# A fourth raw weight buffer, loads one unit earlier, and one scratch tag shared by three uses

## The chip, the cores and the metric

The kernel runs on one core of one Trainium2 chip. The metric is the device time of one launch in microseconds; of the kernel before there are three timed runs, 1531.43, 1519.66 and 1522.27 us, with a median of 1522.27 us. A separate execution was profiled: it took 1527.95 us, of which the profile shows a span of 1526.2 us.

## The reference

Two layers of a hybrid encoder over 256 tokens of width 2048 in float32, each a pre-norm mixer with a residual, then a final RMS norm. Cut to what matters:

```python
u = rms_norm(x, norm_g)
qk, v, o, z_a, ig, fg, xb, z_b = split(u @ w_in)          # w_in: 2048 x 12304
qk = silu(causal_dwconv(qk, qk_conv))                      # 4 taps
q, k = split(qk); k = k * DK_A ** -0.5
h = mlstm_chunkwise(q, k, v, i_pre, log_f)                 # 8 heads, DK 128, DV 256
y_a = group_norm(h * sigmoid(o)) * head_norm_g * silu(z_a)
xc = causal_dwconv(xb, lru_conv_w) + lru_conv_b
y_b = rg_lru(xc, w_a, b_a, w_x, b_x, lam) * silu(z_b)      # gates: sigmoid(xc @ w_a), sigmoid(xc @ w_x)
return x + concat([y_a, y_b]) @ w_out                      # w_out: 4096 x 2048
```

The weights of a layer are read once, some 100 MB in float32 and its `w_out` 33 MB; the products must hold nearly float32's accuracy.

## The kernel before, in words

**Weights.** All weights are laid out in HBM as units of 128 x 2048 floats (1 MB). A unit is loaded by SyncE's queue into a raw buffer (`load_unit`, pool `wraw`, tag `raw`, three buffers). Each half of it (128 x 1024) is then split in two: ScalarE casts the raw half to the TensorE's float32r format, `wH` (L337), and VectorE subtracts to get the rest, `wL` (L338, which the profile shows under the helper's line L187). The pairs H and L have four buffers (pool `wsp`). TensorE multiplies each half as three products, H by H, H by L and L by H (L361): twelve matmuls of 512 columns a half, 24 a unit. A raw buffer is free when `wL` of its second half is done.

**Order.** The main loop at the end of `tile_trunk` walks over the halves. For the half n it first prepares (casts and subtracts) up to half n + 3, and ahead of each preparation it issues loads. With `(nprep + 5) // 2` it has, ahead of the first half of unit m, loaded up to unit m + 2; that load takes the buffer of unit m - 1, whose last subtraction has just been issued. After each half `pump` advances generators that hold the rest of the work (convolutions, gates, scores, the recurrence); a generator that yields "wait" lets the next one go on. Every engine carries out its own instructions in the order in which the program puts them; ScalarE and VectorE thus share one line each between the splits of the weights and the rest.

**Groups.** Each layer has four head groups g. Of a group the projections o, qk, v, xb, z and zb are made, some in another order, then the gates of the recurrence; chunks of `w_out` of the group before are put between. For two of the projections (z of g = 2, o of g = 3) a seven-product block scheme is used, whose summed weights are made by DMAs that add in HBM: GpSimd issues them (`w_d`, L1032), and SyncE's queue reads the sums back as raw units (`raw<-w_d`, L297). A unit of this scheme makes six matmuls a half, twelve in all (`ps_b`, L1095 to L1097). Turning a token-major result into channels goes through HBM too: four DMAs `moved<-blk` on SyncE's queue (L481), one `fr<-moved` on GpSimd's (L482).

**Scratch tiles.** Tiles of the pool `work` with one tag share one buffer: a new tile waits until all that reads the old one is done. The diff is about two tags of 8 KB a partition each. `qs` holds `qks`, the split q and k of a group (L667; read by the score matmuls `ps_S`, L682 and L684), and at the end of layer 0 `tokblk`, the token block and its transpose for the chunks c = 1 and 3 (L942). `xcs` holds `scs`, the rows of the input and forget gates once a layer (L541; last read by GpSimd's copies into `at`, L591, after which the program notes `("aT", l)`), and `xcs`, the split convolution of xb of a group (L768; read by the gate matmuls `ps_gt`, L795).

Of the kernel before, what the change touches and what calls it, by code (L numbers as in the profile page):

```python
# [9 lines left out]
F32 = mybir.dt.float32  # L10
# [83 lines left out]
def tile_trunk(ctx, tc, x, xt, par, gw, gb, ws, final_g, out):  # L94
# [1 line left out]
    V, S, G, PE = nc.vector, nc.scalar, nc.gpsimd, nc.tensor  # L96

    const = ctx.enter_context(tc.tile_pool(name="const", bufs=1))
    wraw = ctx.enter_context(tc.tile_pool(name="wraw", bufs=3))
    wsp = ctx.enter_context(tc.tile_pool(name="wsp", bufs=4))  # L100
    act = ctx.enter_context(tc.tile_pool(name="act", bufs=1))
    work = ctx.enter_context(tc.tile_pool(name="work", bufs=1))
# [547 lines left out]
    def qk_post(l, g, acc):  # L650
        bg.append(e_gen(l, g))
        fr = to_channels(l, acc)

        def gen():
            for _ in range(LANDING):
                yield "wait"
            ch = joined(fr)
            yield 0.3
            qc = work.tile([P, 4, T], F32, tag="c4", name="qc", bufs=2)
            sg = work.tile([P, 4, T], F32, tag="sC", name="qsg")  # L660
            for ct in range(4):
                conv(ch, qc, ct, O_QKW + 4 * (8 * (ct % 2) + 2 * g + ct // 2), l, None)
                yield 1.2
            S.activation(out=sg, in_=qc, func=AF.Sigmoid)
            tt_(qc, qc, sg, ALU.mult)
            yield 1.2
            q = work.tile([P, 4, 2, T], F32R, tag="qs", name="qks")  # L667
            S.copy(out=q[:, :, 0, :], in_=qc)
            tt_(q[:, :, 1, :], qc, q.bitcast(F32)[:, :, 0, :], ALU.subtract)
            yield 1.2  # L670
            for _ in range(3):
                yield "wait"
            while any((k, l, g) not in st for k in ("E", "v", "so")):
                yield "wait"
            E, em, so, (vH, vL) = st["E", l, g], st["em", l], st["so", l, g], st["v", l, g]
            Pt = work.tile([P, 2, 384], F32, tag="ch", name="Pt")
            for h in range(2):
                pa, pb = aux("ps_S"), aux("ps_S")
                kH, kL = q[:, 2 * h + 1, 0], q[:, 2 * h + 1, 1]
                for ps, ss_, ts_1 in ((pa, slice(0, 128), slice(0, 256)), (pb, slice(128, 256), slice(128, 256))):  # L680
                    n_ = ts_1.stop - ts_1.start
                    PE.matmul(ps[:, 0 : 2 * n_].rearrange("p (a t) -> p a t", a=2), kH[:, ss_], q[:, 2 * h, :, ts_1],  # L682
                              start=True, stop=False, skip_group_check=True)
                    PE.matmul(ps[:, 0:n_], kL[:, ss_], q[:, 2 * h, 0, ts_1], start=False, stop=True,  # L684
                              skip_group_check=True)
                for ps, o_, n_ in ((pa, 0, 256), (pb, 256, 128)):
                    S.copy(out=Pt[:, h, o_ : o_ + n_], in_=ps[:, n_ : 2 * n_])
                    tt_(Pt[:, h, o_ : o_ + n_], ps[:, 0:n_], Pt[:, h, o_ : o_ + n_], ALU.add)
                stt(Pt[:, h, :], Pt[:, h, :], DK_SCALE, E[:, h, :], ALU.mult, ALU.mult)
                yield 0.5  # L690
            PH = work.tile([P, 2, 384], F32R, tag="sD", name="PH")
            PL = work.tile([P, 2, 384], F32R, tag="sC", name="PL")
            S.copy(out=PH, in_=Pt)
            tt_(PL, Pt, PH.bitcast(F32), ALU.subtract)
            yield 1.0
            for _ in range(3):
                yield "wait"
            hh = work.tile([P, 2, 2, 256], F32, tag="sE", name="hh")
            mv = small.tile([P, 2, 2, 2], F32, tag="mv", name="mv", bufs=1)
            for h in range(2):  # L700
                pns = [aux("ps_n") for _ in range(2)]
                for t in range(2):
                    o = pns[t][:, 0:258]
                    a = slice(P * t, P * t + P)
                    mm3(o, PH[:, h, a], PL[:, h, a], vH[:, 0, h, :], vL[:, 0, h, :], last=t == 0)
                    if t == 1:
                        mm3(o, PH[:, h, 256:384], PL[:, h, 256:384], vH[:, 1, h, :], vL[:, 1, h, :], first=False)
                for t in range(2):
                    pn = pns[t]
                    dn = small.tile([P, 1], F32, tag="dn", name="dn")  # L710
                    stt(dn, pn[:, 256:257], -1.0, em[:, t, 2 * g + h : 2 * g + h + 1], ALU.mult, ALU.max)
                    tt_(dn, dn, pn[:, 256:257], ALU.max)
                    V.reciprocal(out=dn, in_=dn)
                    stt(hh[:, t, h, :], pn[:, 0:256], dn, so[:, t, 256 * h : 256 * h + 256], ALU.mult, ALU.mult)
                    bs = small.tile([P, 6], F32, tag="bs", name="bs")
                    V.bn_stats(out=bs, in_=hh[:, t, h, :])
                    V.bn_aggr(out=mv[:, t, h, :], in_=bs)
                    yield 1.1
            sd = small.tile([P, 2, 2], F32, tag="sd", name="sd", bufs=1)
            order(S.activation(out=sd, in_=mv[:, :, :, 1], func=AF.Sqrt, bias=epst), st["wH"])  # L720
            V.reciprocal(out=sd, in_=sd)
            for hd in range(2):
                for t in range(2):
                    ts_(hh[:, t, hd, :], hh[:, t, hd, :], mv[:, t, hd, 0:1], ALU.subtract, sd[:, t, hd : hd + 1],
                        ALU.mult)
            st["hn", l, g] = hh
            yield 1.0
        bg.append(gen())
# [30 lines left out]
    def xb_post(l, g, acc):  # L759
        fr = to_channels(l, acc)  # L760

        def gen():
# [2 lines left out]
            ch = joined(fr)  # L765
            yield 0.3
            xc = work.tile([P, 4, T], F32, tag="c4", name="xc", bufs=2)
            xs = work.tile([P, 4, 2, T], F32R, tag="xcs", name="xcs")  # L768
            for ct in range(4):
                tix = 4 * g + ct  # L770
                conv(ch, xc, ct, O_LW + 4 * tix, l, pars[:, l, O_LB + tix : O_LB + tix + 1])
                yield 1.2
            for b in range(2):
                sl_ = slice(2 * b, 2 * b + 2)
                S.copy(out=xs[:, sl_, 0, :], in_=xc[:, sl_, :])
                tt_(xs[:, sl_, 1, :], xc[:, sl_, :], xs.bitcast(F32)[:, sl_, 0, :], ALU.subtract)
                yield 0.6
# [142 lines left out]
    def out_chunk(l, g, c):  # L920
# [9 lines left out]
        def postfn():  # L930
# [8 lines left out]
                new_xT()  # L939
                load_gw(l + 1)  # L940
            if c % 2:
                two = work.tile([P, 2, 1024], F32, tag="qs", name="tokblk")  # L942
                tok = two[:, 0].rearrange("p (m c t j) -> p m c t j", m=4, c=4, t=2)
                blk = two[:, 1].rearrange("p (m n) -> p m n", m=4)
            else:
# [374 lines left out]
    for n, hf in enumerate(order_):  # L1320
        st["n"] = n
        while nprep < len(order_) and nprep <= n + AHEAD:
            while st["nload"] < len(order_) // 2 and st["nload"] <= (nprep + 5) // 2:
                load_unit(order_[2 * st["nload"]])
            prepare(order_[nprep])
            nprep += 1
# [107 lines left out]
```

## Time and profile before

| | |
|---|---|
| median of three runs | 1522.27 us (1519.66 to 1531.43) |
| profiled execution, and its span | 1527.95 us, 1526.2 us |
| TensorE busy | 1489.4 us, 98% |
| VectorE busy | 1140.2 us, 75% |
| ScalarE busy | 966.2 us, 63% |
| DMA moved | 383.44 MB, 251 GB/s in the mean |
| mean granted TensorE clock | 0.993 |

Busy time is what the profile saw an engine work; matmuls are pipelined and overlap in it, so that TensorE can be busy without being at its best pace. A wait names an engine and what it waited for, in total microseconds, the number of times and the longest. In rows of the timeline, what stands in brackets is the idle time of the engine just ahead of the instruction and who ended it. A row of a window holds the stretch, its length, then busy time and count for TensorE, its weight loads, VectorE, ScalarE and GpSimd, the granted TensorE clock, the share of the 16 DMA engines and GB/s.

### The profile page before, as it was taken

What the parts mean: (1) busy time and instruction counts of PE and PEld (TensorE: products, weight loads), DVE (VectorE), ACT (ScalarE), POOL (GpSimd) and SP (SyncE); (2) the same over time, 40 slices, a digit from 0 to 9 for tenths busy, and PEclk for the clock granted to TensorE, in tenths of its full rate; (3) what the DMA queues carried; (4) which work ended last, traced back from release to release, by engine and by line L of the source; (5) the groups of instructions that cost most, each with busy time, mean ns of one, the idle gap of its engine ahead of it and who ended that gap; (6) DMA issues with size and microseconds to landing.
All of it is one profiled execution on the core that took longest, in us unless ns stands there. A gap on an engine that the chain in (4) does not pass through costs nothing.

```text
span 1526.2 us, 18815 instructions
## 1 busy us (share of the span) xinstructions
PE 1489.4 (98%) x6782; PEld 1229.3 (81%) x6782; DVE 1140.2 (75%) x1634; ACT 966.2 (63%) x1258; POOL 107.5 (7%) x186
## 2 busy tenths in 40 slices
PE   9999989999999999999999998999999999999997
PEld 7887768878788878788888787788887888788886
DVE  5879967668867875587867899775986578757785
ACT  6656765557556675568575558654675567755675
POOL 0020010010000100000000200100000000000002
PEclk9999999999999999999999999999999999999999
DMA  9779787897879998976785674978778688677773
GB/s 339 275 256 264 244 284 213 260 288 250 243 279 304 259 279 273 298 238 241 255 296 193 210 263 152 291 216 263 235 247 286 227 236 238 224 236 264 245 265 121
DMA packets 100014, 383.44 MB, mean 251 GB/s; under 512 B 10944, under 2 KB 31440, under 8 KB 76880
## 3 DMA queue, kind: packets, MB, share of 16 engines
q1 hardware_dynamic: 83504, 327.41, 61.6%
q0 software_dynamic: 13952, 50.35, 15.4%
q10 hardware_dynamic: 2464, 4.47, 0.8%
q8 instruction: 53, 0.87, 0.2%
q14 instruction: 41, 0.34, 0.1%
HBM read 344.95 MB, written 62.41 MB: 267 GB/s over the span
## 4 chain that ended last, share of the span: by engine, by line
PE 66%; DMA 12%; DVE 10%; issue 8%; ACT 3%; SPq 0%; POOL 0%; DVEq 0%; ACTq 0%; POOLq 0%
PE acc L361 54%; DMA raw<-in_ws_dram 8%; DVE wL L187 4%; PE ps_gt L795 2%; ACT wH L337 2%; PE acc L374 1%; DMA nb<-nG_d 1%; PE ps_b L1097 1%; PE ps_b L1096 1%; PE ps_b L1095 1%; DMA fr<-moved 1%; DVE xc L190 1%; PE acc L1193 1%; PE acc L1191 1%; PE acc L1192 1%
## 5 line engine op out<-in xcount | busy, mean ns | idle before, releaser
L361 PE MATMUL acc<-wH,x_s 128*128 128x512 f32 x2752 | 860.9, 391 | 7.3 <-ACT wH L337 7.3
L187 DVE TENSOR_TENSOR wL<-raw,wH 128x1024 fp32r<-128x1024 f32 (+1 forms) x556 | 663.3, 1204 | 267.2 <-ACT wH L337 265.5
L337 ACT CAST wH<-raw 128x1024 fp32r<-128x1024 f32 (+1 forms) x556 | 569.7, 1037 | 373.3 <-PE acc L361 252.1
L361 PEld LDWEIGHTS acc<-wH,x_s 128*128 128x128 f32 x2752 | 518.3, 189 | 116.8 <-ACT wH L337 10.2
L361 PE MATMUL acc<-wL,x_s 128*128 128x512 f32 x1376 | 538.6, 392 | 12.5 <-DVE wL L187 12.4
L361 PEld LDWEIGHTS acc<-wL,x_s 128*128 128x128 f32 x1376 | 259.5, 189 | 73.9 <-DVE wL L187 20.4
L361 PE MATMUL acc<-wH,yaH 128*128 128x512 f32 x224 | 87.6, 391 | 0.0
L361 PE MATMUL acc<-wH,yaL 128*128 128x512 f32 x224 | 87.4, 390 | 0.0
L361 PE MATMUL acc<-wL,ybH 128*128 128x512 f32 x224 | 87.3, 390 | 0.0
L361 PE MATMUL acc<-wH,ybL 128*128 128x512 f32 x224 | 87.3, 390 | 0.0
L361 PE MATMUL acc<-wL,yaH 128*128 128x512 f32 x224 | 87.2, 389 | 0.0
L361 PE MATMUL acc<-wH,ybH 128*128 128x512 f32 x224 | 87.2, 389 | 0.0
L478 DVE STREAM_TRANSPOSE blk<-tok 128x1024 f32<-128x1024 f32 x33 | 40.9, 1240 | 21.3 <-ACT tok L468 21.3
L482 POOL DMA_DIRECT2D fr<-moved x34 | 19.0, 560 | 466.6 <-DMA moved<-blk 335.7
L795 PE MATMUL ps_gt<-xcs,wH 128*128 128x256 f32 x256 | 46.9, 281 | 3.2 <-DVE xcs L187 2.0
L361 PEld LDWEIGHTS acc<-wH,ybL 128*128 128x128 f32 x224 | 42.0, 188 | 9.0 <-DVE ybL L187 0.3
L361 PEld LDWEIGHTS acc<-wL,ybH 128*128 128x128 f32 x224 | 42.0, 188 | 8.9 <-DVE wL L187 0.3
L361 PEld LDWEIGHTS acc<-wH,yaL 128*128 128x128 f32 x224 | 42.0, 188 | 8.8
L361 PEld LDWEIGHTS acc<-wH,yaH 128*128 128x128 f32 x224 | 42.2, 188 | 8.4
L361 PEld LDWEIGHTS acc<-wH,ybH 128*128 128x128 f32 x224 | 42.0, 188 | 8.6
L361 PEld LDWEIGHTS acc<-wL,yaH 128*128 128x128 f32 x224 | 42.1, 188 | 8.3
L190 DVE SCALAR_TENSOR_TENSOR qc<-ch,pars,qc 128x255 f32<-128x255 f32 (+2 forms) x96 | 41.4, 478 | 5.0 <-ACT qc L450 4.7
(234 smaller groups left out, 1580.5 us busy)
## 6 DMA issues: line engine op xcount, KB each, us to landing
raw<-in_ws_dram SPq DMA_DIRECT2D x164, 1024.0 KB, 6.2
raw<-in_ws_dram SPq DMA_DIRECT2D x190, 512.0 KB, 6.2
fr<-moved POOLq DMA_DIRECT2D x34, 512.0 KB, 5.8
moved<-blk SPq DMA_DIRECT2D x132, 128.0 KB, 2.8
w_d<-in_ws_dram POOLq DMA_DIRECT2D x32, 512.0 KB, 12.1
raw<-w_d SPq DMA_DIRECT2D x16, 1024.0 KB, 6.7
x_d<-stage POOLq DMA_DIRECT2D x24, 512.0 KB, 6.6
w_d<-in_ws_dram SPq DMA_DIRECT2D x16, 512.0 KB, 7.7
```

Source lines behind the costliest of these rows:

```text
L187: return V.tensor_tensor(out=o, in0=a, in1=b, op=op)
L190: return V.scalar_tensor_tensor(out=o, in0=a, scalar=s, in1=b, op0=op0, op1=op1)
L337: st["wH"] = S.copy(out=H[:, o], in_=r[:, o])
L361: st["mm"] = PE.matmul(o, a_[:, kt, P * t : P * t + P], W[:, k], start=b, stop=z)
L374: PE.matmul(ps[:, ct, T * part : 2 * T], W[:, k, P * ct : P * ct + P], moving, start=first and k == 0 and part == 0, stop=last and k == 3 ...
L478: V.transpose(out=blk.rearrange("p m n -> p (m n)"), in_=tok.rearrange("p m c t j -> p (m c t j)"))
L482: i0 = back.dma_start(out=fr.rearrange("p a c t i -> p a (c t i)"), in_=moved)
L795: PE.matmul(o, W[:, ib, jl], xs[:, ib, a, :], start=j == 0 and i == 0 and W is Hv and a == 0, stop=i == 1 and W is Lv, skip_group_check=True)
L1095: PE.matmul(box["b"], aH, Hv[:, k], start=kp == 0 and k == 0, stop=False)
L1096: PE.matmul(box["b"], aH, Lv[:, k], start=False, stop=False)
L1097: PE.matmul(box["b"], aL, Hv[:, k], start=False, stop=kp == 3 and k == 1)
L1191: PE.matmul(o, yH[:, kt, tsl], Hv[:, k, cs], start=start and k == 0, stop=False)
```

## The change

The pool of raw buffers gets four buffers, and the loop loads one unit further ahead: ahead of the first half of unit m, up to unit m + 3. Its buffer is again that of unit m - 1. The 8 KB a partition for it come from the tag `qs`, which is given up: `qks` and `tokblk` now use the tag `xcs`, with `scs` and the split convolution. So that tiles of this tag follow each other in a set order, the generator that makes `qks` goes on only once `("aT", l)` is noted, and the one that makes the split convolution of a group asks for its tile after the convolution instead of before, and only once the scores of the group have been issued.

```diff
-    wraw = ctx.enter_context(tc.tile_pool(name="wraw", bufs=3))
+    wraw = ctx.enter_context(tc.tile_pool(name="wraw", bufs=4))
...
-            q = work.tile([P, 4, 2, T], F32R, tag="qs", name="qks")
+            while ("aT", l) not in st:
+                yield "wait"
+            q = work.tile([P, 4, 2, T], F32R, tag="xcs", name="qks")
...
+            st["scores", l, g] = True
             PH = work.tile([P, 2, 384], F32R, tag="sD", name="PH")
...
             xc = work.tile([P, 4, T], F32, tag="c4", name="xc", bufs=2)
-            xs = work.tile([P, 4, 2, T], F32R, tag="xcs", name="xcs")
             for ct in range(4):
                 tix = 4 * g + ct
                 conv(ch, xc, ct, O_LW + 4 * tix, l, pars[:, l, O_LB + tix : O_LB + tix + 1])
                 yield 1.2
+            while ("scores", l, g) not in st:
+                yield "wait"
+            xs = work.tile([P, 4, 2, T], F32R, tag="xcs", name="xcs")
...
-                two = work.tile([P, 2, 1024], F32, tag="qs", name="tokblk")
+                two = work.tile([P, 2, 1024], F32, tag="xcs", name="tokblk")
...
-            while st["nload"] < len(order_) // 2 and st["nload"] <= (nprep + 5) // 2:
+            while st["nload"] < len(order_) // 2 and st["nload"] <= (nprep + 7) // 2:
                 load_unit(order_[2 * st["nload"]])
```

The order of the instructions follows. On SyncE's queue, around the fifth group of DMAs that hand a block over (`moved<-blk`), early in layer 0 (`raw` is a raw unit, L306 and L297 two ways of loading one), before:

```order
L306 DMA raw<-in_ws_dram 128x2048
L481 DMA moved<-blk 32x4x256 x4
L306 DMA raw<-in_ws_dram 128x2048
L297 DMA raw<-in_ws_dram 128x2048
L306 DMA raw<-in_ws_dram 128x2048 x3
```

and now:

```order
L306 DMA raw<-in_ws_dram 128x2048
L481 DMA moved<-blk 32x4x256 x4
L297 DMA raw<-in_ws_dram 128x2048
L306 DMA raw<-in_ws_dram 128x2048 x3
```

The unit that was loaded right behind the hand-over is now loaded ahead of it, and the one of L297 stands in its place: the sequence of loads is shifted by one unit against everything else on this queue.

On TensorE, where the loads of those rows are used (`ps_b` is the block scheme, whose unit is the one of L297; `acc<-wH,x_s` behind its first row belongs to the unit after it), before:

```order
L361 MATMUL acc<-wH,x_s 128x512
L1095 MATMUL ps_b<-wH,x_s 128x512
L361 MATMUL acc<-wH,x_s 128x512
L1096 MATMUL ps_b<-wL,x_s 128x512
L1097 MATMUL ps_b<-wH,x_s 128x512
```

and now:

```order
L361 MATMUL acc<-wH,x_s 128x512
L1100 MATMUL ps_b<-wH,x_s 128x512
L1101 MATMUL ps_b<-wL,x_s 128x512
L1102 MATMUL ps_b<-wH,x_s 128x512
L1100 MATMUL ps_b<-wH,x_s 128x512
```

The first matmul of the next unit stood second in the block unit's twelve; now it follows the last of them.

On GpSimd, at the switch from layer 0 to layer 1 (`scs` are the gate rows of layer 1, `gwp` the gate weights, `fr` a block that comes back as channels, `vL` a part of v), before:

```order
L935 DMA x_d_98<-stage 128x1024
L935 DMA x_d_99<-stage 128x1024
L566 MEMSET scs 64x256
L482 DMA fr<-moved 128x1024
L641 MEMSET vH 128x4x2
L482 DMA fr<-moved 128x1024 x2
L521 MEMSET gwp 128x832 x2
L482 DMA fr<-moved 128x1024 x2
L642 MEMSET vL 128x4x2
```

and now:

```order
L940 DMA x_d_98<-stage 128x1024
L940 DMA x_d_99<-stage 128x1024
L482 DMA fr<-moved 128x1024
L641 MEMSET vH 128x4x2
L482 DMA fr<-moved 128x1024 x2
L521 MEMSET gwp 128x832 x2
L482 DMA fr<-moved 128x1024 x2
L566 MEMSET scs 64x256
L642 MEMSET vL 128x4x2
```

The clearing of the gate rows has moved from ahead of the block hand-overs to behind them, since `tokblk` now stands in that buffer until then. On ScalarE and VectorE the casts, the subtractions and the instructions beside them change places here and there along the whole program, mostly by one or two rows.

## The prediction

> **What bounds the kernel.** I read the page first, then the waits, TensorE's groups, the chain of waits, and last the timeline and the granted clock at the places where TensorE stood. The page has the frame:
>
> ```profile
> span 1526.2 us, 18815 instructions
> PE 1489.4 (98%) x6782; PEld 1229.3 (81%) x6782; DVE 1140.2 (75%) x1634; ACT 966.2 (63%) x1258; POOL 107.5 (7%) x186
> ```
>
> TensorE is busy for all but 36.8 us of the span (1526.2 less 1489.4), so no change that leaves the matmuls alone can be worth much more than that. What a deeper ring of raw buffers can take away is the wait for weights. The waits show it on ScalarE, whose cast is the first to touch a raw unit, and, in the queue's own waits, on SyncE:
>
> ```profile
> ACT wH L337 <- DMA raw<-in_ws_dram: 95.4, 48, 6.2
> ...
> SPq L306 <- DVE wL L187: 462.7, 123, 9.4
> ```
>
> ScalarE stood 95.4 us for raw units, 48 times. And the loads themselves stood for the subtraction that frees a buffer, so a fourth buffer does let them go earlier. But ScalarE is busy only 63% of the span, and most of its waits end ahead of TensorE's need. TensorE's own groups show how little arrives there:
>
> ```profile
> L361 PE MATMUL acc<-wH,x_s 128*128 128x512 f32 x2752 | 860.9, 391 | 7.3 <-ACT wH L337 7.3
> L361 PE MATMUL acc<-wL,x_s 128*128 128x512 f32 x1376 | 538.6, 392 | 12.5 <-DVE wL L187 12.4
> ```
>
> 19.7 us of its idle time (7.3 and 12.4) ended with a cast or a subtraction of weights. The question is which part of it had a late transfer behind it.
>
> **The ring, before and after.** The chain of waits gives TensorE's pace and the transfers that lay on the path:
>
> ```profile
> 210.48 14.73 DMA raw<-in_ws_dram
> ...
> 323.53 11.54 DMA raw<-in_ws_dram
> ...
> 396.03 11.29 DMA raw<-in_ws_dram
> ...
> 480.56 16.32 PE acc L361 x72
> ...
> 624.97 13.76 DMA raw<-in_ws_dram
> ...
> 1042.77 21.76 PE acc L361 x96
> ```
>
> 72 matmuls are three units, so a unit takes 5.44 us (16.32 / 3), and 96 matmuls are four, 21.76 us. A buffer is taken up by its transfer and then by two casts and two subtractions; the row of 335.16 below shows the cast begin, and 336.24 with 2.36 us the subtractions end, 3.4 us later. Three buffers turn round at TensorE's pace while a transfer takes under 16.32 - 3.4 = 12.9 us, four under 21.76 - 3.4 = 18.4 us. All transfers of raw units, by the view of that tile, took
>
> ```profile
> DMA to landing us min/median/max: 3.8/6.2/14.9
> ```
>
> from issue to landing. The median needs no fourth buffer; the tail, 11 to 15 us, fills three (the two of 11 us came late as well, since a subtraction stands in VectorE's order behind other work), and not four. Bytes and events that release a load stay as they are: each load waits for the same subtraction as before and brings the next unit.
>
> **Where TensorE stood for it.** The timeline, with the idle time in brackets:
>
> ```profile
> 220.28 2.00 ACT L337 CAST wH<-raw 128x1024 fp32r<-128x1024 f32 x2 [6.17 <-DMA raw<-in_ws_dram]
> ...
> 226.41 0.80 PE L361 MATMUL acc<-wH,x_s 128*128 128x512 f32 x1 [4.04 <-ACT wH L337]
> ...
> 335.16 2.00 ACT L337 CAST wH<-raw 128x1024 fp32r<-128x1024 f32 x2 [5.56 <-DMA raw<-in_ws_dram]
> 336.24 2.36 DVE L187 TENSOR_TENSOR wL<-raw,wH 128x1024 fp32r<-128x1024 f32 x2 [5.38 <-ACT wH L337]
> 337.52 0.50 PE L361 MATMUL acc<-wL,x_s 128*128 128x512 f32 x1 [0.62 <-DVE wL L187]
> ...
> 409.77 0.50 PE L361 MATMUL acc<-wL,x_s 128*128 128x512 f32 x1 [0.73 <-DVE wL L187]
> ...
> 638.88 1.99 ACT L337 CAST wH<-raw 128x1024 fp32r<-128x1024 f32 x2 [5.73 <-DMA raw<-in_ws_dram]
> ...
> 639.97 0.50 PE L361 MATMUL acc<-wH,x_s 128*128 128x512 f32 x1 [0.77 <-ACT wH L337]
> 641.23 0.60 PE L361 MATMUL acc<-wL,x_s 128*128 128x512 f32 x1 [0.76 <-DVE wL L187]
> ```
>
> Four places, one behind each of the four long transfers above: 4.04 + 0.62 + 0.73 + (0.77 + 0.76) = 6.92 us idle. Two of them cost more, because TensorE's clock fell behind them. By windows (granted clock is the third number from the right):
>
> ```profile
> 225.00:228.00 3.00, 1.59 (x4) 1.30 (x5) 0.00 (x0) 2.69 (x3) 0.00 (x0) 0.51 0.99 392
> 228.00:231.00 3.00, 3.00 (x9) 2.32 (x8) 2.71 (x3) 1.89 (x3) 0.00 (x0) 0.50 0.25 107
> 231.00:234.00 3.00, 3.00 (x13) 2.44 (x12) 3.00 (x4) 1.90 (x3) 0.00 (x0) 0.85 0.42 79
> ...
> 639.00:642.00 3.00, 1.47 (x4) 0.81 (x4) 2.05 (x2) 2.51 (x3) 0.00 (x0) 0.91 1.05 431
> 642.00:645.00 3.00, 3.00 (x9) 2.32 (x8) 2.67 (x3) 1.35 (x2) 0.00 (x0) 0.52 0.74 219
> ```
>
> What a slow clock costs is the missing share times the length: (0.49 + 0.50 + 0.15) x 3 = 3.42 us at the first place, (0.09 + 0.48) x 3 = 1.71 us at the second. Idle time and clock together: 6.92 + 5.13 = 12.05 us.
>
> [...]
>
> **The change part by part.** The loads: what one unit's lead is worth is 5.44 us at TensorE's pace, against waits of at most 6.2 us. The place of the 4.04 us is the hardest, since its loads were issued close together:
>
> ```profile
> 208.21 0.35 SPq L297 DMA_DIRECT2D raw<-in_ws_dram  x1
> ...
> 207.00:228.00 21.00, 16.95 (x72) 13.69 (x71) 12.94 (x19) 11.18 (x14) 2.75 (x4) 0.93 1.01 315
> ```
>
> The late unit, issued at 210.48 and landed 14.73 us later, goes in the changed order at the place of the load of 208.21, so it lands by 222.9 even if it takes as long. On TensorE the matmul that stood for it, second among the twelve of the block unit, now comes behind them: the first of the twelve ended at 226.41 - 4.04 = 222.4, eleven more at 5.44 / 24 take 2.5 us, to 224.9. TensorE began 1.2 us after the landing (226.41 less 210.48 and 14.73), which now makes 224.1. So the 4.04 us go, and the clock with them. The other three places have 5.44 us of lead against waits of 5.56, 5.73 and less: what is left is 0.3 us, and I set it at nothing. Value of the loads: 12.05 us; bounds 6.9 (idle time alone, if short gaps elsewhere drag the clock down in their place) and 20 (below, the third case).
>
> At the start nothing is won: from 5 to 45 us the DMA engines are full,
>
> ```profile
> 5.00:45.00 40.00, 40.00 (x173) 32.26 (x172) 24.07 (x43) 28.89 (x59) 0.00 (x0) 1.00 1.02 378
> ```
>
> and the fourth unit and the token loads behind it stand in the same order in one queue. At the end the loads have long been issued.
>
> The shared tag costs a wait only where a tile's last reader is later than the next tile's first writer. The tightest places, in order of time:
>
> ```profile
> 83.95 4.16 POOL L591 COPY at<-scs 32x16 f32<-32x16 f32 x8
> ...
> 99.83 1.05 ACT L668 CAST qks<-qc 128x1024 fp32r<-128x1024 f32 x1 [0.35 <-DVE qc L187]
> ...
> 117.03 0.22 PE L684 MATMUL ps_S<-qks 128*128 128x128 f32 x1
> ...
> 127.91 0.61 ACT L775 CAST xcs<-xc 128x512 fp32r<-128x512 f32 x1
> ```
>
> The gate rows are read until 88.1, the split q and k begins at 99.8: 11.7 us to spare. The scores are read until 117.3, the split convolution begins at 127.9: 10.7 us. The later groups and the token block have more, so the tag waits for nothing and I cost it at 0; what is queued behind such a wait on ScalarE are the weight casts, and its price is in the fourth case. The clearing of the gate rows, moved behind the hand-overs on GpSimd, has only a memset of v, one hand-over and the gate rows' own DMA behind it, far from the end of any chain: 0.
>
> The other places that change by a row or two on ScalarE and VectorE: no row shows the new order, and the nearest is a place where two casts stood behind gate work,
>
> ```profile
> 543.00:546.00 3.00, 1.46 (x5) 1.01 (x6) 3.00 (x3) 2.97 (x4) 1.44 (x2) 0.98 0.75 240
> 546.00:549.00 3.00, 3.00 (x9) 2.32 (x8) 3.00 (x5) 2.21 (x4) 0.00 (x0) 0.50 0.95 201
> ```
>
> It costs 1.54 us idle and (0.02 + 0.50) x 3 = 1.56 us of clock, 3.1 us. The new order can make one such place or undo one: from +3.1 to -3.1 us, and I take 0.
>
> **The sum.** 1527.95 - 12.05 = 1515.9 us for an execution like the profiled one. That one lies 5.7 us above the median of 1522.27; the runs spread over 11.8 us, as much as the term itself, and late transfers are the likeliest thing to differ between runs. Taken off the median the term gives 1510.2. If the 5.7 us are part of it, 1515.9 is the median itself. I take the middle, 1513 us, 0.6% less.
>
> **The rivals.** *The burst only moves the wait.* In the window from 207 to 228 us the DMA engines are full. What is short there is the rate and not the lead, and TensorE stands one unit later for as long. For it: a share of 1.01 through 21 us. Against it: the median transfer takes 6.2 us, so there is slack around the burst to fill a buffer. SyncE's queue may also stand for earlier transfers instead of for a buffer,
>
> ```profile
> SPq L304 <- DMA raw<-in_ws_dram: 19.5, 13, 3.4
> ```
>
> and then the loads don't get ahead at all, and the change doesn't do what it says. Either way nothing is won: 1522 us. [...]
>
> *More is won.* ScalarE's 95.4 us of waits held back convolutions and scores too. TensorE's waits for casts and subtractions that no transfer explains are 19.7 - 6.92 = 12.8 us; if half of them go, and with them the slow clock of two places like the one at 546 (1.56 us each), 9.5 us more are gone: 1513 - 9.5 = 1503.5 us. Against it: where VectorE is full its work is the bound,
>
> ```profile
> 900.00:925.00 25.00, 21.56 (x103) 17.55 (x103) 24.82 (x67) 16.56 (x23) 0.11 (x1) 1.00 0.51 177
> ```
>
> and no lead helps there.
>
> *The shared tag binds: slower.* If the scores of a group end later than its convolution, the split convolution stands on ScalarE, with the weight casts behind it. The place at 638.88 has the price: ScalarE stood 5.73 us and TensorE lost 0.77 + 0.76 + 1.71 = 3.24 us. In all eight groups that is 25.9 us, 1539 us; in half of them 1526. It decides from the point where the 10.7 us of slack are used up; the profile shows no group near that, but a new order of the scores could do it.
>
> **How the numbers follow.** The forecast has a chance of 0.58, nothing won 0.18, more won 0.12, the tag 0.12. One per cent is 15.2 us, and about what a measurement of this kernel can tell from no change: under 1507.0 is faster, over 1537.5 slower. Of "more won" 0.10 lie under 1507.0, of the forecast 0.04: faster 0.14. Of the tag 0.04 lie over 1537.5: slower 0.04. The rest, 0.82, is within 1%. The range from 1503 to 1524 us takes in the forecast's bounds (1510 to 1516, and 3.1 us on either side for the order), nothing won, and most of "more won"; it leaves out the tag and the ends, about 0.18.
>
> **What would show it.** Right: ScalarE's waits for raw units fall from 95.4 us to under 30; the granted clock stays full around 225 and 642 us; TensorE's idle time before L361 falls by about 7 us; the casts of q and k and of the convolution wait for no gate row and no score. Wrong: long raw waits at the same places one unit later (the burst); new waits of ScalarE in front of the split convolution (the tag); a clock that falls at as many places as before, if elsewhere.

## The result, and the profile after

The changed kernel takes 1511.88 us (median of 16 runs, 1509.5 to 1519.08), the kernel before 1521.15 us beside it. The ratio is 0.9937, with a 95% interval from 0.9922 to 0.9952: 9.3 us faster (7.3 to 11.9), inside one per cent. The forecast was 1513 us. The profiled execution took 1512.39 us.

The head of the page of the changed kernel, to be set against 1526.2 and 1489.4 us:

```profile
span 1510.7 us, 18798 instructions
PE 1484.0 (98%) x6782; PEld 1227.8 (81%) x6782; DVE 1142.3 (76%) x1634; ACT 967.9 (64%) x1258; POOL 106.7 (7%) x186
```

TensorE is not busy for 26.7 us (1510.7 less 1484.0) instead of 36.8. Its own busy time is 5.4 us less although its instructions are the same ones. In the kernel before a matmul of 512 columns counts 0.63 us busy at a granted clock of 0.50 (227.00 to 231.27 us) and 0.39 us at 1.00 (232.02 us), and by an estimate 3.6 of the 5.4 us are that: summed over the span, the share missing from the granted clock comes to 10.6 us before and 7.0 us now. The waits of the changed kernel (total us, times, longest us):

```profile
ACT wH L337 <- PE acc L361: 310.4, 225, 5.4
ACT wH L337 <- DMA raw<-in_ws_dram: 18.3, 14, 2.9
```

ScalarE's waits for raw units went from 95.4 to 18.3 us. Its waits for TensorE to free a buffer of split weights went from 252.1 to 310.4 us. So 77 us less for loads stand against 58 us more for TensorE: most of these casts were off the critical path, and end a wait for a load only to wait for TensorE. TensorE's two groups of L361 (the last part is idle time, and what ended most of it):

```profile
L361 PE MATMUL acc<-wH,x_s 128*128 128x512 f32 x2752 | 860.1, 391 | 3.2 <-ACT wH L337 3.0
L361 PE MATMUL acc<-wL,x_s 128*128 128x512 f32 x1376 | 537.6, 392 | 9.8 <-DVE wL L187 9.7
```

Casts and subtractions end 12.7 us of idle time (3.0 and 9.7) instead of 19.7. The view of the raw tile tells that the transfers did not get shorter:

```profile
DMA to landing us min/median/max: 3.8/6.1/14.3
```

14.3 us after 14.9. They are covered instead. In the chain of waits of the changed kernel, raw transfers are left at the start (the last two of them shown), and two short ones later:

```profile
24.12 9.09 DMA raw<-in_ws_dram
...
33.22 11.19 DMA raw<-in_ws_dram
...
123.64 4.41 DMA raw<-in_ws_dram
...
529.69 4.97 DMA raw<-in_ws_dram
```

And by windows, at the two places where the clock had fallen (busy TensorE is the first number behind the length, the granted clock the third from the right), TensorE is busy all the time at the full clock:

```profile
225.00:228.00 3.00, 3.00 (x15) 2.49 (x14) 3.00 (x4) 2.74 (x4) 0.00 (x0) 1.00 0.98 360
228.00:231.00 3.00, 3.00 (x14) 2.46 (x14) 2.99 (x4) 1.76 (x2) 0.00 (x0) 1.00 1.03 410
...
639.00:642.00 3.00, 3.00 (x15) 2.22 (x14) 3.00 (x8) 1.84 (x3) 0.00 (x0) 1.00 0.88 294
642.00:645.00 3.00, 3.00 (x15) 2.49 (x14) 2.64 (x4) 1.89 (x2) 0.57 (x1) 1.00 0.90 233
```

Something came, too. At 94 us the changed kernel has a stall that the kernel before has not. In its timeline:

```profile
94.19 1.01 DVE L195 TENSOR_SCALAR E<-nb,at 128x256 f32<-128x256 f32 x4 [5.53 <-DMA nb<-nG_d]
95.11 1.22 DVE L187 TENSOR_TENSOR wL<-raw,wH 128x1024 fp32r<-128x1024 f32 x1
...
96.39 0.50 PE L361 MATMUL acc<-wL,x_s 128*128 128x512 f32 x1 [1.84 <-DVE wL L187]
```

VectorE waits 5.53 us for the gate rows to come back from HBM (`nb`), a subtraction of weights stands behind that in its order, and TensorE waits for the subtraction. In the kernel before, the rows were there sooner:

```profile
90.75 1.02 DVE L195 TENSOR_SCALAR E<-nb,at 128x256 f32<-128x256 f32 x4 [4.32 <-DMA nb<-nG_d]
```

The way of the gate rows to HBM (`nG_d<-scs`, 8 KB) and back is what differs. The last number is the time from issue to landing, before:

```profile
nb<-nG_d POOLq DMA_DIRECT2D x1, 256.0 KB, 7.2
nG_d<-scs POOLq DMA_DIRECT2D x1, 8.0 KB, 2.0
```

and after:

```profile
nb<-nG_d POOLq DMA_DIRECT2D x1, 256.0 KB, 4.9
nG_d<-scs POOLq DMA_DIRECT2D x1, 8.0 KB, 5.2
```

The write is issued at 83.74 us instead of 81.16, since VectorE's order has a part of the convolution of q and k ahead of the rows now, and it takes 3.2 us longer. This comes with the fourth buffer and not with the tag: below, the tag alone leaves the order and the write (2.2 us) as they were, and TensorE stands 0.31 us there; the buffer without the earlier load has the new order and stalls of 2.02 and 2.69 us. Behind the stall the clock falls, as the window of the changed kernel shows:

```profile
98.00:101.00 3.00, 3.00 (x9) 2.39 (x8) 2.96 (x5) 2.86 (x3) 0.58 (x1) 0.55 0.45 111
```

### The profile page after: what moved, and what is told of

Its sections match the earlier page's. It is cut to its first block, busy times and chain, and to the rows that moved or that the text cites. A ratio compares the mean times of both kernels' runs of the same rounds, so it can differ in the third digit from the quotient of the medians.

```text
span 1510.7 us, 18798 instructions
## 1 busy us (share of the span) xinstructions
PE 1484.0 (98%) x6782; PEld 1227.8 (81%) x6782; DVE 1142.3 (76%) x1634; ACT 967.9 (64%) x1258; POOL 106.7 (7%) x186
## 4 chain that ended last, share of the span: by engine, by line
PE 79%; issue 8%; DVE 6%; DMA 5%; ACT 2%; SPq 0%; POOL 0%; POOLq 0%; DVEq 0%; ACTq 0%
PE acc L361 66%; DMA raw<-in_ws_dram 3%; DVE wL L187 2%; PE ps_gt L800 2%; PE ps_b L1101 2%; PE ps_b L1102 2%; PE ps_b L1100 1%; PE acc L374 1%; DMA nb<-nG_d 1%; ACT wH L337 1%; PE acc L1197 1%; PE acc L1196 1%; PE acc L1198 1%; PE ps_S L684 0%; DMA nG_d<-scs 0%
## 5 line engine op out<-in xcount | busy, mean ns | idle before, releaser
L361 PE MATMUL acc<-wH,x_s 128*128 128x512 f32 x2752 | 860.1, 391 | 3.2 <-ACT wH L337 3.0
L337 ACT CAST wH<-raw 128x1024 fp32r<-128x1024 f32 (+1 forms) x556 | 572.0, 1038 | 366.1 <-PE acc L361 310.4
L361 PEld LDWEIGHTS acc<-wH,x_s 128*128 128x128 f32 x2752 | 518.3, 189 | 112.0 <-ACT wH L337 5.3
L361 PE MATMUL acc<-wL,x_s 128*128 128x512 f32 x1376 | 537.6, 392 | 9.8 <-DVE wL L187 9.7
L361 PEld LDWEIGHTS acc<-wL,x_s 128*128 128x128 f32 x1376 | 259.3, 188 | 68.4 <-DVE wL L187 15.0
L361 PE MATMUL acc<-wH,yaH 128*128 128x512 f32 x224 | 87.3, 390 | 0.0
L361 PE MATMUL acc<-wH,yaL 128*128 128x512 f32 x224 | 87.3, 390 | 0.0
L361 PE MATMUL acc<-wL,ybH 128*128 128x512 f32 x224 | 87.3, 390 | 0.0
L361 PE MATMUL acc<-wH,ybL 128*128 128x512 f32 x224 | 87.3, 390 | 0.0
L361 PE MATMUL acc<-wH,ybH 128*128 128x512 f32 x224 | 87.2, 389 | 0.0
L361 PE MATMUL acc<-wL,yaH 128*128 128x512 f32 x224 | 87.2, 389 | 0.0
L361 PEld LDWEIGHTS acc<-wH,ybL 128*128 128x128 f32 x224 | 42.1, 188 | 9.1 <-DVE ybL L187 0.3
L361 PEld LDWEIGHTS acc<-wL,ybH 128*128 128x128 f32 x224 | 42.0, 188 | 8.9 <-DVE wL L187 0.3
L361 PEld LDWEIGHTS acc<-wH,yaL 128*128 128x128 f32 x224 | 42.0, 188 | 8.6
L361 PEld LDWEIGHTS acc<-wH,ybH 128*128 128x128 f32 x224 | 42.0, 188 | 8.6
L361 PEld LDWEIGHTS acc<-wH,yaH 128*128 128x128 f32 x224 | 42.1, 188 | 8.4
L361 PEld LDWEIGHTS acc<-wL,yaH 128*128 128x128 f32 x224 | 42.1, 188 | 8.3
L939 ACT COPY stage<-acc 128x1024 f32<-128x1024 f32 x24 | 24.4, 1016 | 37.3 <-PE acc L361 34.8
```

The lines of the kernel that those rows point to most:

```text
L337: st["wH"] = S.copy(out=H[:, o], in_=r[:, o])
L361: st["mm"] = PE.matmul(o, a_[:, kt, P * t : P * t + P], W[:, k], start=b, stop=z)
L939: S.copy(out=stage, in_=ps)
```

## The experiments

The theory was that of the prediction: the fourth buffer covers transfers of 11 to 15 us, the burst of transfers makes these long, and the shared tag costs nothing. The rivals: the gain comes from another part of the change (the order on TensorE, the tag's waits); the late transfers are only the bad luck of one profiled execution; the wait moves elsewhere.

**The tag alone.** The changed kernel with three buffers and the old lead:

```diff
-    wraw = ctx.enter_context(tc.tile_pool(name="wraw", bufs=4))
+    wraw = ctx.enter_context(tc.tile_pool(name="wraw", bufs=3))
...
-            while st["nload"] < len(order_) // 2 and st["nload"] <= (nprep + 7) // 2:
+            while st["nload"] < len(order_) // 2 and st["nload"] <= (nprep + 5) // 2:
```

> The shared tag and its two waits alone, with three buffers and the old lead. The matmuls stand in the same order as before. If the gain is the lead's (theory) the tag costs and gains nothing: ratio to before 0.998 to 1.002, ScalarE's waits for raw units 80 to 110 us as before. If the tag's order brings the gain: 0.994. If the tag binds and the buffer pays for it: over 1.003, with new waits in front of the split convolution or of the split q and k.

Measured: 1522.29 us, ratio 1.0001 (0.9985 to 1.0017). Its waits for raw units are still there:

```profile
ACT wH L337 <- DMA raw<-in_ws_dram: 83.3, 42, 6.5
```

The tag neither costs nor gains anything beyond this interval of 0.2% (some 3 us). What it gives is the space.

**The order on TensorE alone.** The kernel before, with the matmul of the next unit kept behind the twelve of the block unit, as the change has it:

```diff
+                    if "pb" in st:
+                        order(st["mm"], st.pop("pb"))
...
-                    PE.matmul(box["b"], aL, Hv[:, k], start=False, stop=kp == 3 and k == 1)
+                    st["pb"] = PE.matmul(box["b"], aL, Hv[:, k], start=False, stop=kp == 3 and k == 1)
```

> The kernel before, three buffers, with one thing of the new order: the first matmul of the unit behind a block unit is kept behind all twelve of the block's matmuls. If the lead makes the gain (theory): 0.997 to 1.000, raw waits of ScalarE 80 to 110 us, with at most the 4 us gap at 222 us shortened to about 1.5 us. If the order at this place is most of the gain (rival): 0.993 to 0.996 with the raw waits unchanged.

Measured: 1522.22 us, ratio 1.0001 (0.9981 to 1.0022). In its timeline the 4.04 us of one gap are spread over several, each still behind a cast or a subtraction:

```profile
221.71 0.50 PE L1098 MATMUL ps_b<-wL,x_s 128*128 128x512 f32 x1 [0.76 <-DVE wL L187]
...
225.64 0.50 PE L361 MATMUL acc<-wH,x_s 128*128 128x512 f32 x1 [1.16 <-ACT wH L337]
228.48 0.79 PE L361 MATMUL acc<-wH,yaH 128*128 128x512 f32 x1 [2.34 <-ACT wH L337]
229.94 0.79 PE L361 MATMUL acc<-wL,x_s 128*128 128x512 f32 x1 [0.67 <-DVE wL L187]
```

They sum to 4.93 us, and the clock falls behind them for 6.8 us as it did before. Moving the matmul that waits doesn't bring the unit.

**The kernel before and the changed one again.** No edit; each takes another profile, which tells what recurs from what one execution happened to have.

> The kernel before, profiled once more: the ratio is 1.000 within 0.2%. If late transfers make its spread between runs, its idle time behind the four long transfers differs from the first profile's 12 us (idle and clock); the raw waits of ScalarE stay at 80 to 110 us.

Measured: 1522.56 us, ratio 1.0004 (0.9985 to 1.0023). The second profile of the kernel before has the same places:

```profile
225.93 0.80 PE L361 MATMUL acc<-wH,x_s 128*128 128x512 f32 x1 [4.28 <-ACT wH L337]
...
639.25 0.50 PE L361 MATMUL acc<-wH,x_s 128*128 128x512 f32 x1 [1.06 <-ACT wH L337]
640.51 0.50 PE L361 MATMUL acc<-wL,x_s 128*128 128x512 f32 x1 [0.76 <-DVE wL L187]
```

with the clock down behind both:

```profile
225.00:228.00 3.00, 2.07 (x5) 1.69 (x6) 0.19 (x1) 2.78 (x3) 0.00 (x0) 0.50 0.89 356
228.00:231.00 3.00, 3.00 (x9) 2.33 (x8) 3.00 (x3) 1.99 (x2) 0.00 (x0) 0.50 0.12 52
...
642.00:645.00 3.00, 3.00 (x9) 2.30 (x9) 2.07 (x2) 0.68 (x2) 0.00 (x0) 0.54 0.88 284
```

So the late transfers are not the bad luck of one execution. What they cost does differ between executions: the profiles with the tag alone and with TensorE's order alone, both with three buffers, have the long transfers at the same places, but there the clock stays full around 642 us.

> The changed kernel once more, as the measure for the three others on the same chip: ratio 0.992 to 0.995, raw waits of ScalarE 15 to 25 us, two or three stretches of half clock inside the run.

> The changed kernel once more, beside the version with the cast put first: 0.992 to 0.995 of the kernel before by either theory. Its stall of about 2 us at 93 us, which the profiles with four buffers show and those with three don't, should be there again (1.9 to 2.8 us), and the pairs of 1.1 and 1.2 us at 534 and 1283 us too.

Measured: 1510.3 us, ratio 0.9922 (0.9894 to 0.9950), and in a later comparison 1511.26 us, 0.9926 (0.9907 to 0.9945). The second of these profiles is of the longest of its six executions, 1517.74 us. The stall near 94 us is in both profiles, in the first as

```profile
95.18 0.50 PE L361 MATMUL acc<-wL,x_s 128*128 128x512 f32 x1 [1.96 <-DVE wL L187]
```

and in the second smaller than expected:

```profile
95.75 0.50 PE L361 MATMUL acc<-wL,x_s 128*128 128x512 f32 x1 [1.19 <-DVE wL L187]
```

The clock did not fall behind it in either; the window from 98 to 101 us of the second:

```profile
98.00:101.00 3.00, 3.00 (x15) 2.48 (x14) 2.96 (x4) 2.63 (x3) 0.00 (x0) 1.00 0.61 187
```

**Two buffers.** The ring sum the other way: with two buffers, a transfer of more than 2 x 5.44 - 3.4 = 7.5 us stands in TensorE's way.

```diff
-    wraw = ctx.enter_context(tc.tile_pool(name="wraw", bufs=3))
+    wraw = ctx.enter_context(tc.tile_pool(name="wraw", bufs=2))
...
-            while st["nload"] < len(order_) // 2 and st["nload"] <= (nprep + 5) // 2:
+            while st["nload"] < len(order_) // 2 and st["nload"] <= (nprep + 3) // 2:
```

> Two raw buffers and a lead one unit shorter, old tags. By the ring's sum two buffers cover a transfer of 10.9 - 3.4 = 7.5 us; a third or more of the transfers are longer, and a block unit needs one in half the time. Theory: raw waits of ScalarE over 300 us, ratio 1.02 to 1.08. If the third buffer were as little needed as the fourth (rival: only the bursts count): 1.005 to 1.01.

Measured: 1662.14 us, ratio 1.0927 (1.0897 to 1.0957), slower than the expected range. Its waits:

```profile
ACT wH L337 <- DMA raw<-in_ws_dram: 378.9, 148, 11.3
...
PE acc L361 <- ACT wH L337: 48.5, 25, 5.3
PE acc L361 <- DVE wL L187: 41.5, 46, 3.9
```

So a third buffer is worth 140 us and a fourth 9. TensorE waits 70.3 us more for casts and subtractions (48.5 + 41.5 less 19.7), and the clock, whose mean is 0.968 there, costs by its missing share some 53 us (0.032 of 1662.4) instead of 10.6; the rest lies in other places. The ring sum does not explain these waits by the length of the transfers: in this kernel their median is 5.1 us, and only 45 of the 325 whose landing is on record took more than 7.5 us, while ScalarE waited 148 times.

**Without the bursts.** The same pair, with three and with four buffers, without the 32 DMAs by which GpSimd adds weights of the block scheme to each other in HBM. The block scheme's sums are left out with them.

```diff
-                    else:
-                        order(G.dma_start(out=wd[l][to][j][:, cs], in_=src, accum_op=ALU.add), st["gq"])
```

> The kernel before without GpSimd's 32 adding DMAs that sum the block scheme's weights (left out; the sums then hold one weight alone). If the bursts of these DMAs make the long transfers (theory): raw waits of ScalarE 30 to 50 us, no transfer of a raw unit over 12 us behind the start, ratio 0.993 to 0.996. If the ring is short without them too (rival): raw waits over 70 us, ratio 0.998 to 1.000.

> The changed kernel without the same 32 adding DMAs (left out). If the fourth buffer does nothing but cover the bursts (theory), it now gains next to nothing over the same kernel with three buffers: ratio to before 0.991 to 0.995, at most 0.2% under that one. If the lead has a gain of its own (rival): 0.4% or more under it.

Measured: 1513.54 us with three buffers, ratio 0.9950 (0.9929 to 0.9971), and 1513.55 us with four, 0.9952 (0.9931 to 0.9972). With three buffers ScalarE's waits for raw units become

```profile
ACT wH L337 <- DMA raw<-in_ws_dram: 30.9, 20, 3.0
```

and, by the view of the raw tile, the transfers

```profile
DMA to landing us min/median/max: 3.7/5.7/11.8
```

The longest transfer, 11.8 us, is under the 12.9 us that three buffers cover, and the fourth buffer gains nothing. Taking the bursts away does for three buffers about as much as a fourth buffer does with the bursts. One reserve: the zero between three and four is a balance. In the two profiles TensorE is not busy for 29.7 us with three buffers and 26.0 with four, but ahead of the end the clock falls once with three (1286 us) and three times with four (97, 537 and 909 us), 1.7 us each. The four-buffer kernel keeps its stall at 94 us here as well, 1.77 us.

**The buffer without the earlier load.** Four buffers, but the lead of the kernel before:

```diff
-            while st["nload"] < len(order_) // 2 and st["nload"] <= (nprep + 7) // 2:
+            while st["nload"] < len(order_) // 2 and st["nload"] <= (nprep + 5) // 2:
```

> Four buffers and the shared tag, but the loop puts each load where it put it before, one unit less ahead. SyncE's queue does nothing but wait at these loads, so if the fourth buffer is what counts (theory) the loads start as early as in the changed kernel: ratio 0.992 to 0.996, raw waits of ScalarE under 30 us. If the place in the program counts: 0.997 to 1.000 and raw waits over 60 us.

Measured: 1515.89 us, ratio 0.9962 (0.9946 to 0.9978). The waits for raw units are gone as with the whole change,

```profile
ACT wH L337 <- DMA raw<-in_ws_dram: 16.8, 13, 2.1
```

and yet a part of the gain is missing: in the same comparison the changed kernel takes 1510.3 us, and the slowest of its six runs (1511.43 us) is faster than the fastest of these twelve (1514.68 us). Neither the theory (the lead is all that counts, and the buffer gives it) nor the rival had this. Its timeline shows where TensorE stands instead:

```profile
206.79 7.13 SPq L306 DMA_DIRECT2D raw<-in_ws_dram  x3
...
207.82 0.56 POOL L482 DMA_DIRECT2D fr<-moved  x1 [6.74 <-DMA moved<-blk]
...
217.81 1.05 ACT L504 COPY ch<-fr 128x1024 f32<-128x1024 f32 x1 [5.51 <-DMA fr<-moved]
...
219.43 4.83 DVE L190 SCALAR_TENSOR_TENSOR qc<-ch,pars,qc 128x255 f32<-128x255 f32 x12 [5.87 <-ACT qc L450]
...
224.18 2.35 DVE L187 TENSOR_TENSOR wL<-raw,wH 128x1024 fp32r<-128x1024 f32 x2
...
225.45 0.50 PE L1101 MATMUL ps_b<-wL,x_s 128*128 128x512 f32 x1 [3.13 <-DVE wL L187]
```

The raw loads are issued from 206.79, ahead of GpSimd's load of a block for the convolution (`fr<-moved`). In the changed kernel this group of raw loads starts at 209.54, behind that load, which is issued at 207.78. The block load, 512 KB, takes

```profile
fr<-moved POOLq DMA_DIRECT2D x1, 512.0 KB, 10.0
```

10.0 us here against 4.2 to 4.4 us in the three profiles of the changed kernel (3.9 before, in both). VectorE waits for the block in order, and the subtraction of weights waits behind the convolution. To see whether that recurs:

> Four buffers with the lead left at five, once more. In its first profile the load of the moved inputs at 207.82 us took 10.0 us instead of 3.9 to 4.6, because three raw loads had been issued just ahead of it (206.79); the copy, the convolution and the weight subtraction behind it on VectorE came late, and TensorE stood 3.13 us at 222. Theory (the place of the raw loads makes this): the load of the moved inputs takes 8 to 12 us again, TensorE stands 2 to 4 us before the block unit at 222 us, and the time is 0.995 to 0.997 of the kernel before. Rival (chance of one execution): that load takes 4 to 5 us, TensorE doesn't stand at 222, and the time is 0.992 to 0.995 as with the whole change.

Measured: 1517.0 us, ratio 0.9969 (0.9949 to 0.9989). The block load took 9.0 us again:

```profile
fr<-moved POOLq DMA_DIRECT2D x1, 512.0 KB, 9.0
```

and TensorE stood 1.61 us for the same subtraction, less than the 2 to 4 us expected. So the place of the loads among the other DMAs looks like a part of the gain: the lead of one unit puts this group of raw loads behind the block load. That a raw load issued ahead of it makes the block load long is read from these rows, twice; it was not tried by moving that one load alone.

**A cast put first.** After the change, the stalls that are left have no transfer behind them. Two pairs are alike, in the third group of each layer; of the changed kernel:

```profile
535.49 0.51 PE L361 MATMUL acc<-wH,x_s 128*128 128x512 f32 x1 [0.94 <-ACT wH L337]
...
536.95 0.50 PE L361 MATMUL acc<-wL,x_s 128*128 128x512 f32 x1 [0.95 <-DVE wL L187]
```

There two casts stand on ScalarE behind a table load, an exponential and a tanh of the gate (1.28, 1.71 and 1.69 us from 529.89 us on). In `gate_post` of the changed kernel:

```diff
+            late = g == 2
+            for _ in range(2 * late):
+                yield "wait"
...
-                order(e, st["sig"])
+                order(e, st["wH"] if late and ct == 0 else st["sig"])
```

> The changed kernel, with one weight cast of ScalarE put ahead of the table load, the exponential and the tanh of the gate in the third group of each layer. After the change TensorE still stands 1.09 + 1.23 us at 534 us and again at 1283 us, where two casts stand behind that gate work, and the half clock at 537.6 us costs another 3.4 us. Theory (the order on ScalarE is what bounds there, and no lead of the loads can help): both pairs of stalls fall under 0.6 us, the half clock at 538 us goes, 2 x 2.3 + 3.4 = 8.0 us at most; 0.989 to 0.992 of the kernel before. Rival (the gate, later by a cast, now holds up its own matmuls or the next casts): the stalls move by a unit, 0.993 to 0.996, as the whole change alone.

> The version with the cast put first, on the same chip as the changed kernel. Theory (the order on ScalarE bounds the places at 534 and 1283 us): 3 to 5 us faster than the changed kernel, 0.988 to 0.992 of the kernel before, and the stall of 3.16 us that its first profile had at 1260 us, behind a load of moved inputs that came late, is not there again. Rival (that stall belongs to this order and gives the gain back): 3 us of stall at 1260 us again, and the time within 2 us of the changed kernel, 0.992 to 0.995.

(The 1.09 and 1.23 us in the expectation are the gaps from start to start beyond TensorE's pace, the 0.94 and 0.95 us above the idle time; the expectation's 3.4 us are the length of the stretch at a clock of 0.50, which costs half of that, 1.7 us.) Measured: 1508.06 us, ratio 0.9906 (0.9885 to 0.9927), and 1507.14 us, ratio 0.9901 (0.9882 to 0.9920), beside 0.9926 for the changed kernel in the same comparison. At 536 us one stall is left:

```profile
536.54 0.50 PE L361 MATMUL acc<-wL,x_s 128*128 128x512 f32 x1 [0.39 <-DVE wL L187]
```

The stalls fell as expected (to 0.39 and 0.38 us in the later pair too), and the half clock at 538 us is gone (1.00 in the window from 537 to 540 us), as is that at 910 us; the mean clock of both profiles is 0.998, against 0.994 to 0.996 in those of the changed kernel. A part came back elsewhere: gate matmuls near 908 us wait 1.44 and 1.45 us in the two profiles, against 0.34 us in the changed kernel. The version's medians lie 3.8 and 4.1 us under those of the changed kernel, but the intervals of the ratios overlap: that it beats the kernel before is shown, that it beats the changed one is likely. The stall of 3.16 us at 1260 us was not in its second profile, and the second additional profile of the changed kernel had one of 2.89 us at the same place:

```profile
1269.37 0.58 PE L361 MATMUL acc<-wL,x_s 128*128 128x512 f32 x1 [2.89 <-DVE wL L187]
```

So that one belongs to single executions, not to this order. Five buffers were not tried, since there is no room for the fifth.

## Why the prediction was right, and where it was not

**The loads, 12.05 us.** The mechanism held. The four places of the chain are gone, in both kinds of rows: the idle time before L361 fell by 7.0 us (19.7 to 12.7), and the clock is full at 225 and 642 us. The size of the term was that of one execution, 5.7 us above the median. The profiles with three buffers, and those of the changed kernel, side by side ("idle" is the span less TensorE's busy time, "half clock" the time at a granted clock of 0.5 ahead of the kernel's end, with the start of each stretch; a stretch costs about half its length: in the kernel before a matmul of 512 columns starts every 0.43 us at 227 us, at a clock of 0.50, and every 0.23 us at 233 us, at 1.00):

| profile | execution, us | idle, us | half clock, us | four places, us |
|---|---|---|---|---|
| before | 1527.95 | 36.8 | 17.1 (225, 546, 642, 959) | 6.9 + 5.1 |
| before, again | 1527.24 | 36.2 | 17.1 (225, 641, 925, 1300) | 6.8 + 5.1 |
| tag alone | 1521.07 | 34.2 | 10.2 (224, 545, 954) | 4.9 + 1.7 |
| TensorE's order alone | 1520.71 | 33.3 | 10.2 (228, 545) | 5.7 + 3.4 |
| changed | 1512.39 | 26.7 | 10.2 (97, 538, 910) | 0 |
| changed, again | 1508.98 | 24.8 | 6.8 (169, 906) | 0 |
| changed, third | 1517.74 | 29.4 | 13.7 (536, 908, 1270, 1290) | 0 |

The last column is idle time and clock at the four places of the prediction. In the mean of the four profiles they cost 9.9 us, not 12.05, and 12.05 only in the two executions that lie 5 us above their median. Means of the other columns: TensorE's idle time fell by 8.1 us (35.1 to 27.0), and half clock by 3.4 us, which is 1.7 us of time. Together that is 9.8 us, against 9.3 us measured (7.3 to 11.9). The forecast had too much clock in it (5.13 us) and somewhat too little idle time (6.92 us).

**The order of ScalarE and VectorE, taken as 0 within 3.1 us either way.** It came out near nothing, but as the sum of several things at places that the prediction didn't look at. Since it had no row for them, the zero was luck. The largest cost is the stall at 94 us, 1.84, 1.96 and 1.19 us in the three profiles of the changed kernel. Behind one of the three the clock fell: by the windows from 95 to 101 us, 0.88 and 0.55, that is (0.12 + 0.45) x 3 = 1.71 us.

```profile
95.00:98.00 3.00, 1.61 (x6) 1.29 (x7) 3.00 (x6) 2.75 (x4) 1.79 (x4) 0.88 0.00 0
```

The prediction named the gate rows' own DMA only at the switch of layers, where it comes early enough; at the start of layer 0, where TensorE waits for it within some 10 us, the same DMA wasn't followed. The largest gain is at the gate matmuls of a later group, before and after:

```profile
924.87 0.39 PE L795 MATMUL ps_gt<-xcs,wH 128*128 128x256 f32 x1 [1.76 <-DVE xcs L187]
```

```profile
915.68 0.39 PE L800 MATMUL ps_gt<-xcs,wH 128*128 128x256 f32 x1 [0.34 <-DVE xcs L187]
```

All four profiles with three buffers have 1.76 to 1.81 us there, all three of the changed kernel 0.34 us. In the first pair of profiles two waits for subtractions near 525 and 1281 us go from 0.67 to 0.29 us as well, and one near 919 us from 1.67 to 1.94. That makes 2.1 us lost (1.84 + 0.27) and 2.2 us won (1.42 + 0.38 + 0.38), without the clock. No wait for a raw unit stands ahead of the three that fell, in the timeline of the kernel before.

**The two readings of the base.** The forecast took the middle between 1515.9 us (the 5.7 us by which the profiled execution lay above the median are a part of the term) and 1510.2 us (they are not). The table says that each is right in part: the first and the last of the four places recur in every profile with three buffers, but the full price stands only in the two executions that lie 5 us above their median. Two of the four profiles are of edited kernels, though of ones whose times do not differ from the kernel before (both ratios 1.0001). The middle was right for the reason given, that late transfers differ between runs; how far to go was a guess. The difference of the two profiled executions, 15.6 us (1527.95 less 1512.39), overstates the gain by what the first of them lay above its median.

**The tag at 0, the start at 0.** Right. The tag alone gives 1.0001. At the start the transfers of 24.12 and 33.22 us stand in the chain as before.

**The ring sum.** It fits where a buffer is to spare: the fourth gains nothing where the longest transfer is 11.8 us, and covers 14.3 us. For two buffers the direction was right and the size too small: with 45 of 325 transfers over 7.5 us, ScalarE waited 148 times. So a buffer must often be held for longer than the 3.4 us that the sum takes for its casts and subtractions. What holds it was not followed.

**The rivals.** *The burst only moves the wait*: false for the whole change, since the waits at those places are gone and not one unit later. The longest transfer stayed as long (14.3 us after 14.9), and the gain came from covering it instead. With the buffer alone the rival is half true: there the block load took 10.0 and 9.0 us instead of 4.2 to 4.4. *More is won*: it did not come as a whole. The 2.2 us above are of its kind, and the stall at 94 us took about as much away. The stalls at 534 and 1283 us stayed, and the last experiment shows that order, not lead, is what they need. *The tag binds*: false.

**The clock.** The prediction counted a fall at the second place, behind gaps of 0.77 and 0.76 us. The second profile of the kernel before has the fall at 642 us again, at 0.54, behind gaps of 1.06 and 0.76 us, and the changed kernel has neither such gaps there nor the fall. That the clock falls behind gaps so short is thus shown twice. But with the tag alone and with TensorE's order alone, where the idle time there is 0.53 and 0.76 us, the clock stays at 1.00: its 1.71 us belong to some executions only.

**What would show it.** ScalarE's raw waits under 30 us (18.3), the full clock at both places, the idle time down by about 7 us (7.0) and no wait for a gate row or a score ahead of the split tiles all came true. Of the signs against it, the last one came in part: the changed kernel's clock falls in two to four stretches ahead of the end, at other places, against two to four with three buffers.

## What to carry to other kernels

A deeper ring of buffers is worth what late transfers cost at the consumer that sets the end, not at the first one that waits: 95.4 us of waits on ScalarE held 12 us of TensorE's time at most. The sum (buffers x time of a unit - time of processing) tells which transfers are late, as long as nothing else holds a buffer. A load issued earlier also moves ahead of, or behind, every small load that other engines wait for, so look for the short DMAs in the new order, above all at the start, before counting them at nothing. And a second profile of the kernel before, of an execution near the median, tells which late transfers recur and at what price; only that belongs in the sum.

## What was not expected of the hardware

Small transfers stretch too. The write of 8 KB took 2.0 and 2.1 us in the two profiles of the kernel before and 4.2 to 5.2 us in the three of the changed one, and the block load of 512 KB took between 3.9 and 10.0 us. The loads of other queues stood beside both; that these stretch them was not tried by moving one alone.

Here the granted clock did not follow the length of one gap. A stall of 1.84 us was followed by a fall to 0.55 in one profile of the changed kernel, and one of 1.96 us by none in another, whose window is

```profile
98.00:101.00 3.00, 3.00 (x14) 2.46 (x14) 3.00 (x4) 2.46 (x4) 0.00 (x0) 1.00 0.87 264
```

The clock records of the first profile of each kernel tell more. Ahead of the kernel's end the stretches of half clock are 3.41 us long, the one at 225 us twice that (6.83), and in each of the two profiles they begin a whole number of steps of 3.413 us after the first one (before: 94, 122 and 215 steps; changed: 129 and 238). The steps lie elsewhere in the two: the first falls, at 225.06 and 97.28 us, are 37.4 steps apart. Laid over TensorE's idle time, these steps go far to tell falls from no falls: each of the seven falls follows a step that holds at least 1.53 us of idle time in sum, and none of the other steps at full clock holds more than 1.69 us. The two steps that come nearest to each other are both of the kernel before, each shown with the step behind it (the idle time is the length less TensorE's busy time):

```profile
638.07:641.48 3.41, 1.88 (x8) 1.03 (x7) 1.53 (x2) 2.12 (x3) 0.00 (x0) 1.00 1.00 397
641.48:644.90 3.42, 3.42 (x9) 2.63 (x9) 3.19 (x3) 1.87 (x2) 0.00 (x0) 0.50 0.80 256
...
921.39:924.80 3.41, 1.72 (x9) 1.10 (x7) 3.41 (x10) 2.22 (x3) 0.00 (x0) 1.00 0.81 267
924.80:928.21 3.41, 3.34 (x28) 3.34 (x29) 3.41 (x6) 2.54 (x5) 0.00 (x0) 1.00 0.00 0
```

The 1.53 us are two gaps, 0.77 and 0.76; the gap of 1.84 us lay within one step; how the 1.96 us of the other profile lay to its steps is not shown. So in these two profiles the falls go with the idle time within one such step, in one gap or in several, and not quite strictly; a fall costs 1.7 us, half of 3.413. No run moved a gap on purpose to test it.
